# Last tiles of a dense expert mixer finished half by half, fetches paced to end earlier, nine more of them in the first pass

## Chip, core and metric

One core of one Trainium2 chip runs the whole program. The metric is the device time of one execution in microseconds, as the median of several runs. TensorE (PE) does matrix products, VectorE (DVE) and ScalarE (ACT) work on 128-partition tiles, GpSimd (POOL) issues the indirect fetches here, and SyncE (SP) issues most other DMAs.

## What is computed

A layer of token mixing is followed by an expert mixer (PEER) over 1024 latent tokens and 16384 experts with one row each in `peer_u` and `peer_v`. The changed part is the expert mixer and the final norm:

```python
def peer_ffn(h, q_w, sub_keys, u_tab, v_tab):
    ...
    top_s, pos = lax.top_k(cand_s, PEER_TOPK)
    idx = jnp.take_along_axis(cand_i, pos, axis=-1)
    gates = jax.nn.softmax(top_s, axis=-1)
    def chunk(args):
        x_c, i_c, g_c = args
        act = jax.nn.gelu(jnp.einsum('chkd,cd->chk', u_tab[i_c], x_c))
        return jnp.einsum('chk,chkd->cd', g_c * act, v_tab[i_c])
    ...
xl = xl + g2 * peer_ffn(hl2, ...)
return rmsnorm(xl, final_g)
```

Each token has 8 heads of 16 experts, so 128 of the 16384 rows count for it.

## The kernel before

The 1024 tokens are 8 tiles of 128. The experts of three of them (`GTILES` 0, 6, 7) are fetched row by row; for the five others (`DTILES` 1 to 5, 640 tokens) every expert is multiplied densely and the gates, mostly zero, select.

**Fetched tiles.** `gathered()` is a generator of 768 steps: for each tile 128 fetches from `peer_u` (`ru`, each followed by a dot product on VectorE, line 1133), then 128 from `peer_v` (`rv`, each followed by a multiply-add into `acc`, line 1144). One step is one indirect DMA on POOL (`rows()`, line 1116) of 128 rows of 1024 floats, 512 KB. Seven buffers (`UVB`) hold fetched rows. `advance(n)` brings the generator to step n, and `paced()` ties each fetch to the latest eviction of the dense work, so the fetches run in step with the products. The numbers in `PACE` set how far: 45 steps come before the first pass, `PACE["u"]` more in it.

**First pass.** For each of 128 blocks of 128 experts, `peer_ut` is loaded (`du`), split in a high part (ScalarE, `duh`) and a low part (VectorE, `dul`), multiplied with the 640 tokens on PE (`ds`, three products each, `mm3`), passed through GELU on ScalarE (`ge`), and stored to `d_ge`. In the last blocks the operands of the second pass begin to be loaded.

**Second pass.** 32 groups of 4 blocks. Per block, `operands()` (line 1218 ff.) loads `dws` from `d_ge` and `dvs` from `peer_v`, multiplies `dws` by the gates `dgs` (one load of 1.25 MB for a group), and splits both (ScalarE `dwhs`, `dvhs`; VectorE `dwls`, `dvls`). PE forms ten results of 128 x 512, two column halves of each of the five tiles, with 12 products each in a group: seven stay in PSUM banks (`stay`, shown as `dp`), and three (`dq`) share one bank, are evicted after each group and added into `dacc` by VectorE. One `advance` belongs to each of the 320 results: fetching ends `VEND` = 8 results before the end.

**The end.** In the last group the ten results are finished in the order `LAST`, and whenever both halves of a tile are there, `finish()` does its part: product with `g2b` (line 1098), addition of the residual row `x1r` (line 1099, on GpSimd for tiles in `EASED`, on VectorE for the others), square and sum on ScalarE (line 1100). The inverse roots (`rsqrt_few`, twelve small VectorE instructions, lines 148 to 154) and the final products (line 1108) come for two tiles together, and then for three (`ENDS`). The fetched tile 7 has a `finish()` of its own at the end of `gathered()`.

What each engine executes is one queue in the order that a scheduler gave it when the program was built; an instruction that waits holds everything behind it on its engine. SP's and POOL's DMA issues are such queues too.

## Time and profile before

| what | value |
| --- | --- |
| median of 3 runs | 3594.12 us (3587.15 to 3605.07) |
| the profiled execution | 3599.58 us, of which the span is 3597.6 us |
| PE busy | 3257.7 us, 91% of the span |
| VectorE busy | 2803.5 us, 78% |
| ScalarE, POOL busy | 1514.4 us (42%), 1364.3 us (38%) |
| chain that ended last | PE 36%, VectorE 5%, DMA 2%, issue 2% |
| HBM traffic | 800.64 MB read, 121.63 MB written |

The shares are means over stages: the mixing part fills the time up to about 1400 us, the first pass runs from there to about 2700 us, the second from there to 3572 us. Which engine limits a stage is read from the busy time of that stage and from what PE waits for in it. A timeline row gives start, duration, engine, line, operation, output and inputs, and, in brackets, the idle time before it and who ended it.

### The profile page before, as it was taken

The numbers are of one execution on the slowest core, as the hardware profiler recorded it, in microseconds if no ns is written. First come the engines' busy times: TensorE is split into PE (matmuls) and PEld (weight loads), VectorE is DVE, ScalarE is ACT, GpSimd is POOL, SyncE is SP. The second block draws the span as 40 slices with busy tenths as digits, with TensorE's granted clock in tenths as the row PEclk, the third lists the DMA queues.
The fourth block names the chain that finished last, engine by engine and source line by source line (L and its number), as shares of the span: only waits on it lengthen the run. The fifth ranks groups of instructions, "written<-read, shape, count | busy, mean of one in ns | idle before, by whom it ended". The sixth has DMA issues, their size and how long they took to land. (4 is left out here: it accounts for less than half of the span.)

```text
span 3597.6 us, 62347 instructions
## 1 busy us (share of the span) xinstructions
PE 3257.7 (91%) x23447; PEld 2906.9 (81%) x23447; DVE 2803.5 (78%) x6117; ACT 1514.4 (42%) x2918; POOL 1364.3 (38%) x1052
## 2 busy tenths in 40 slices
PE   6788989977788879899899999999978999999996
PEld 5566777766788668899899999999966888888885
DVE  6654554466578579798889999997769988888888
ACT  3543333232465332363436667666522333233322
POOL 3332233231111233554423335465545445444433
PEclk8899999987899889999999999999998999999998
DMA  7434435352553546999878789999999999999996
GB/s 256 139 101 141 147 105 153 93 152 78 166 157 113 181 162 230 326 321 323 298 272 279 279 285 359 359 360 352 335 350 370 372 352 350 359 344 345 356 344 235
DMA packets 404718, 926.39 MB, mean 258 GB/s; under 512 B 45504, under 2 KB 182080, under 8 KB 398784
## 3 DMA queue, kind: packets, MB, share of 16 engines
q1 hardware_dynamic: 246976, 406.71, 35.4%
q0 software_dynamic: 111920, 407.95, 31.1%
q10 hardware_dynamic: 45520, 107.76, 7.7%
q8 instruction: 184, 3.01, 0.3%
q14 instruction: 118, 0.97, 0.1%
HBM read 800.64 MB, written 121.63 MB: 256 GB/s over the span
## 5 line engine op out<-in xcount | busy, mean ns | idle before, releaser
L1116 POOL DMA_INDIRECT ru<-in_peer_u_dram,idx x384 | 519.4, 1353 | 637.2 <-ACT dqs L1350 152.9
L1116 POOL DMA_INDIRECT rv<-in_peer_v_dram,idx x384 | 502.5, 1309 | 667.2 <-ACT dqs L1350 187.3
L1144 DVE SCALAR_TENSOR_TENSOR acc<-rv,gw,acc 128x1024 f32<-128x1024 f32 x381 | 488.3, 1282 | 25.7 <-DMA rv<-in_peer_v_dram,idx 21.7
L1133 DVE CUSTOM_DVE_ANT_0 ru<-ru,h 128x1024 f32<-128x1024 f32 x384 | 461.2, 1217 | 50.5 <-DMA ru<-in_peer_u_dram,idx 50.2
L160 PE MATMUL dp<-dvls,dwhs 128*128 128x512 f32 x896 | 347.8, 391 | 0.0
L161 PE MATMUL dp<-dvhs,dwls 128*128 128x512 f32 x896 | 346.1, 390 | 0.0
L209 POOL TENSOR_TENSOR wl<-w,wh 128x1024 fp32r<-128x1024 f32 x68 | 165.7, 2439 | 385.0 <-ACT wh L207 363.8
L159 PE MATMUL dp<-dvhs,dwhs 128*128 128x512 f32 x896 | 248.7, 396 | 0.2 <-ACT dvhs L1231 0.2
L159 PE MATMUL pj<-hbh,wh 128*128 128x512 f32 (+1 forms) x544 | 216.8, 399 | 16.6 <-ACT hbh L189 14.7
L160 PE MATMUL pj<-hbl,wh 128*128 128x512 f32 (+1 forms) x544 | 212.3, 390 | 3.9 <-POOL hbl L190 3.9
L1265 ACT ACTIVATE ge<-ds 128x256 f32<-128x256 f32 (+1 forms) x256 | 110.7, 433 | 247.0 <-PE ds L161 222.6
L161 PE MATMUL pj<-hbh,wl 128*128 128x512 f32 (+1 forms) x544 | 211.1, 388 | 2.3 <-POOL wl L209 2.3
L159 PEld LDWEIGHTS dp<-dvhs,dwhs 128*128 128x128 f32 x896 | 171.5, 192 | 36.2 <-ACT dvhs L1231 0.6
L160 PEld LDWEIGHTS dp<-dvls,dwhs 128*128 128x128 f32 x896 | 169.3, 189 | 35.4
L161 PEld LDWEIGHTS dp<-dvhs,dwls 128*128 128x128 f32 x896 | 169.2, 189 | 35.3
L1235 ACT CAST dwhs<-dws 128x640 fp32r<-128x640 f32 x128 | 91.9, 730 | 233.5 <-DVE dws L1234 205.0
L159 PE MATMUL dq<-dvhs,dwhs 128*128 128x512 f32 x384 | 152.1, 396 | 32.6 <-ACT dvhs L1231 26.0
L727 POOL TENSOR_TENSOR kl<-kd,kh 128x768 fp32r<-128x768 f32 (+1 forms) x24 | 55.0, 2290 | 319.2 <-ACT kh L725 293.0
L1231 ACT CAST dvhs<-dvs 128x1024 fp32r<-128x1024 f32 x128 | 134.0, 1051 | 91.6 <-DMA dvs<-in_peer_v_dram 91.5
L207 ACT CAST wh<-w 128x1024 fp32r<-128x1024 f32 x68 | 71.0, 1046 | 234.6 <-PE pj L160 169.8
L1350 ACT COPY dqs<-dq 128x512 f32<-128x512 f32 x90 | 52.8, 587 | 276.9 <-PE dq L161 276.9
L1048 PE MATMUL gm<-oa,ob 128*128 128x128 f32 x1280 | 159.1, 277 | 3.6 <-DVE oa L1035 3.0
(1980 smaller groups left out, 10123.5 us busy)
## 6 DMA issues: line engine op xcount, KB each, us to landing
du<-in_peer_ut_dram SPq DMA_DIRECT2D x128, 512.0 KB, 6.4
dvs<-in_peer_v_dram SPq DMA_DIRECT2D x128, 512.0 KB, 7.0
d_ge<-ge ACTq DMA_DIRECT2D x128, 320.0 KB, 5.4
d_g<-gt ACTq DMA_DIRECT2D x40, 1024.0 KB, 10.5
dgs<-d_g SPq DMA_DIRECT2D x32, 1280.0 KB, 9.4
dws<-d_ge SPq DMA_DIRECT2D x128, 320.0 KB, 8.2
w<-in_w_in_dram SPq DMA_DIRECT2D x68, 512.0 KB, 3.6
wq<-in_q_w_dram SPq DMA_DIRECT2D x48, 512.0 KB, 4.0
```

What stands on the lines that cost most here:

```text
L159: nc.tensor.matmul(ps, lh_, rh_, start=start, stop=False)
L160: nc.tensor.matmul(ps, lh_, rl_, start=False, stop=False)
L161: nc.tensor.matmul(ps, ll_, rh_, start=False, stop=stop)
L207: nc.scalar.copy(wh, w)
L209: WE[0].tensor_tensor(wl, w, wh.bitcast(F32), op=OP.subtract)
L1048: nc.tensor.matmul(ps[:, t * P:(t + 1) * P], ob[:, q + t], oa[:, q + t], start=True, stop=True)
L1116: paced(nc.gpsimd.indirect_dma_start(out=r, out_offset=None, in_=A[tab], in_offset=bass.IndirectOffsetOnAxis(ap=idx[:, tt, s:s + 1], axis=0)))
L1133: yield from rows("peer_u", tt, lambda s, u: nc.vector.tensor_tensor_reduce(u, u, h2, 1.0, 0.0, OP.mult, OP.add, act[:, s:s + 1]))
L1144: nc.vector.scalar_tensor_tensor(acc, v, w[:, s:s + 1], acc, op0=OP.mult, op1=OP.add)
L1231: nc.scalar.copy(vh, v)
L1235: nc.scalar.copy(wh, wt)
L1265: ev = nc.scalar.activation(ge[:, t0:t0 + n], ps, AF.Gelu_apprx_tanh)
```

## The change

Three numbers change and the end is rewritten.

- `PACE["u"]` goes from 450 to 459: nine more fetch steps in the first pass, nine fewer in the second.
- `VEND` goes from 8 to 17: fetching ends nine results sooner. In the second pass 288 steps (with the 15 of `LAG`) over 312 results become 279 over 303.
- In the last group each half of a dense tile is finished as soon as its products are done (`half_done`): product with `g2b`, addition of `x1r` (on VectorE always), square and sum of 512 columns on ScalarE. The second half of a tile adds the two sums, takes one inverse root for that tile, and does the final product and the store to HBM in two halves. GpSimd adds nothing any more, and `ENDS` and `EASED` are gone.

```diff
--- before.py
+++ after.py
@@ -38,15 +38,13 @@
 GROUPS = ((0, 256), (256, 512), (768, 256))
 DBLK = ((0, 256), (256, 384))
 EB, VB = 4, 7
-PACE = dict(g0=5, g1=(40,), u=450)
+PACE = dict(g0=5, g1=(40,), u=459)
 REST = (16, 2)
 HTOK, TOKS, IBLK = 32, 8, 64
 GSTEPS = TD // TOKS
-VEND = 8
+VEND = 17
 SEAM = 6
-ENDS = ((0, 4), (1, 2, 3))
 LAG = 15
-EASED = (1, 5, 7)
 LAST = (7, 0, 8, 1, 9, 2, 3, 4, 5, 6)
 HP = (600, 500)
 BESIDE = 1.2
@@ -1086,8 +1084,6 @@
         sm, accs = pl.tile([P, 2 * n], F32, tag=f"sm{n}", name=f"sm{tts[0]}", bufs=2), []
 
         def wide(nm, tt):
-            if late and nm == "fin" and tt in DTILES:
-                return late[2][DTILES.index(tt)]
             return ex.tile([P, D], F32, tag="uv", name=f"{nm}{tt}", bufs=UVB)
 
         for i, tt in enumerate(tts):
@@ -1096,7 +1092,7 @@
             for q, part in enumerate(parts[i]()):
                 d_ = slice(q * 512, (q + 1) * 512)
                 nc.vector.tensor_mul(acc[:, d_], part, g2b[:, d_])
-            (nc.gpsimd if late and tt in EASED else nc.vector).tensor_add(acc, acc, x1r)
+            nc.vector.tensor_add(acc, acc, x1r)
             nc.scalar.activation(x1r, acc, AF.Square, accum_out=sm[:, i:i + 1])
             accs.append(acc)
             yield
@@ -1300,6 +1296,27 @@
 
     old = dgs[NGRP % 2].rearrange("p c i t -> p (c i t)")
     late.append([old[:, :D], old[:, D:2 * D], dqs.rearrange("p a b -> p (a b)")] + fins_)
+
+    def half_done(got, i):
+
+        (t, q), part = divmod(i, 2), stay[i] if i < len(stay) else dacc[:, i - len(stay)]
+        tt, d_ = DTILES[t], slice(q * 512, (q + 1) * 512)
+        both = t in got
+        if not both:
+            x1r = ex.tile([P, D], F32, tag="uv", name=f"x1r{tt}", bufs=UVB)
+            nc.sync.dma_start(x1r, d_x1[tt * P:(tt + 1) * P, :])
+            got[t] = (x1r, late[2][t], dn.tile([P, 4], F32, tag="smd", name=f"smd{tt}", bufs=TD // P))
+        x1r, acc, sm = got[t]
+        nc.vector.tensor_mul(acc[:, d_], part, g2b[:, d_])
+        nc.vector.tensor_add(acc[:, d_], acc[:, d_], x1r[:, d_])
+        nc.scalar.activation(x1r[:, d_], acc[:, d_], AF.Square, accum_out=sm[:, q:q + 1])
+        if both:
+            nc.vector.tensor_add(sm[:, 2:3], sm[:, 0:1], sm[:, 1:2])
+            rsqrt_few(dn, sm[:, 3:4], sm[:, 2:3], 1, 1e-6, 1.0 / D, "fn1")
+            for d_ in (slice(0, 512), slice(512, D)):
+                nc.vector.scalar_tensor_tensor(acc[:, d_], acc[:, d_], sm[:, 3:4], late[0][:, d_], op0=OP.mult, op1=OP.mult)
+                nc.sync.dma_start(out[tt * P:(tt + 1) * P, d_], acc[:, d_])
+
     for g in range(NGRP):
         if g:
             ws.clear()
@@ -1322,7 +1339,7 @@
         left_ = GT * 2 * P - n1
         steps = NGRP * NT2 - VEND
         if g == NGRP - 1:
-            fins, fgen, ends = (), None, list(ENDS)
+            got = {}
             for x, i in enumerate(LAST):
                 if i < len(stay):
                     acc_of(i, stay[i], False, True)
@@ -1331,15 +1348,7 @@
                     acc_of(i, ps, True, True)
                     nc.vector.tensor_add(dacc[:, i - len(stay)], ps, dacc[:, i - len(stay)])
                 advance(n1 - LAG + (g * NT2 + x + 1) * (left_ + LAG) // steps)
-                if (i ^ 1) in LAST[:x]:
-                    if not fins:
-                        fins = ends.pop(0)
-                        fgen = finish([DTILES[t] for t in fins], [lambda t=t: [stay[j] if j < len(stay) else dacc[:, j - len(stay)] for j in (2 * t, 2 * t + 1)] for t in fins])
-                    assert fins[0] == i // 2
-                    next(fgen)
-                    fins = fins[1:]
-                    if not fins:
-                        drain(fgen)
+                half_done(got, i)
             break
         for r in range(nr):
             ps = bank(f"dq{g}{r}", "ch")
```

What the scheduler makes of it shows in three places. In the rows, the number behind an underscore is a buffer's serial number.

The first is VectorE at the end. Before, the last three fetched rows (`rv7_125` to `rv7_127`) stand between the finishing steps of the dense tiles and ahead of the addition of the ninth result (`dq318`):

```order
L1098 TENSOR_TENSOR dgs0_27653<-dp3_28065,g2b_9644 128x512
L1144 SCALAR_TENSOR_TENSOR acc7_31320<-rv7_125_33797,gw7_31317,acc7_31320 128x1024
L1098 TENSOR_TENSOR dqs_28082<-dp4_28066,g2b_9644 128x512
L1144 SCALAR_TENSOR_TENSOR acc7_31320<-rv7_126_33843,gw7_31317,acc7_31320 128x1024
L1144 SCALAR_TENSOR_TENSOR acc7_31320<-rv7_127_33858,gw7_31317,acc7_31320 128x1024
L1332 TENSOR_TENSOR dacc_28069<-dq318_33861,dacc_28069 128x512
L1098 TENSOR_TENSOR fin7_33893<-acc7_31320,g2b_9644 128x512 x2
L1098 TENSOR_TENSOR dqs_28082<-dp5_28067,g2b_9644 128x512
L1098 TENSOR_TENSOR fin1_28084<-dacc_28069,g2b_9644 128x512
L1098 TENSOR_TENSOR fin0_28083<-dp6_28068,g2b_9644 128x512
L1332 TENSOR_TENSOR dacc_28069<-dq319_33923,dacc_28069 128x512
```

Now the last fetched rows stand ahead of the last group's operands (`dvls0`, `dvls1`), and tile 7 is finished (`fin7`) before the last group's products:

```order
L1140 SCALAR_TENSOR_TENSOR acc7_31162<-rv7_125_33707,gw7_31159,acc7_31162 128x1024
L1360 TENSOR_TENSOR dacc_28096<-dqs_28109,dacc_28096 128x512
L1140 SCALAR_TENSOR_TENSOR acc7_31162<-rv7_126_33710,gw7_31159,acc7_31162 128x1024
L1140 SCALAR_TENSOR_TENSOR acc7_31162<-rv7_127_33713,gw7_31159,acc7_31162 128x1024
L1094 TENSOR_TENSOR fin7_33761<-acc7_31162,g2b_9644 128x512 x2
L1228 TENSOR_TENSOR dvls0_27687<-dvs0_27683,dvhs0_27686 128x1024
L1095 TENSOR_TENSOR fin7_33761<-fin7_33761,x1r7_33760 128x1024
L1232 TENSOR_TENSOR dwls1_27689<-dws1_27682,dwhs1_27688 128x640
L1228 TENSOR_TENSOR dvls1_27691<-dvs1_28114,dvhs1_27690 128x1024
```

Fetched rows have left the stretch in which the dense tiles are finished.

Behind the last result (`dq319`, the tenth) VectorE has now the following; the roots of two tiles (`smd5` and `smd2`) then alternate instruction by instruction:

```order
L1349 TENSOR_TENSOR dacc_28096<-dq319_33957,dacc_28096 128x512
L152 SCALAR_TENSOR_TENSOR smd1_33898<-fn1t_33940,fn1y_33939 128x1
L1314 TENSOR_TENSOR smd3_34061<-smd3_34061 128x1
L1314 TENSOR_TENSOR smd4_33880<-smd4_33880 128x1
L1310 TENSOR_TENSOR fin1_28111<-dacc_28096,g2b_9644 128x512
L1317 SCALAR_TENSOR_TENSOR dgs0_27680<-dgs0_27680,smd1_33898,fgs_28088 128x512 x2
L1311 TENSOR_TENSOR fin1_28111<-fin1_28111,x1r5_33916 128x512
L1314 TENSOR_TENSOR smd5_33918<-smd5_33918 128x1
L146 TENSOR_SCALAR fn1a_33975<-smd5_33918 128x1
L146 TENSOR_SCALAR fn1a_34028<-smd2_34008 128x1
```

The five dense tiles' final products (`L1108` before, 1024 columns each) have become halves that stand behind the root of their own tile.

The second place is SP's queue between the passes. Before, after the last `dvs` loads of group 0, the gates of group 1 (`dgs1`) come first and the load of its first block (`dws1`) behind them:

```order
L1218 DMA dvs0_27656<-in_peer_v_dram 128x1024 x2
L1218 DMA dgs1_28085<-d_g_79 128x20x128
L1218 DMA dws1_27655<-d_ge_78 128x640
L1218 DMA dvs0_27656<-in_peer_v_dram 128x1024
L1218 DMA dws2_28086<-d_ge_78 128x640
L1218 DMA dvs1_28087<-in_peer_v_dram 128x1024
```

Now three loads of group 1 stand ahead of its gates:

```order
L1214 DMA dvs0_27683<-in_peer_v_dram 128x1024 x2
L1214 DMA dws1_27682<-d_ge_78 128x640
L1214 DMA dvs0_27683<-in_peer_v_dram 128x1024
L1214 DMA dws0_27681<-d_ge_78 128x640
L1214 DMA dgs1_28112<-d_g_79 128x20x128
L1214 DMA dws2_28113<-d_ge_78 128x640
```

The gates of group 1 have moved back behind `dws1`, `dvs0` and `dws0`.

The third is ScalarE at the end of the first pass. Before, the high part of block 124 is cast behind the second GELU of block 123:

```order
L1265 ACTIVATE ge122_27594<-ds122_256_27621 128x384
L1267 DMA d_ge_78<-ge122_27594 128x640
L1059 CAST du123h_27692<-du123_27690 128x1024
L1265 ACTIVATE ge123_27696<-ds123_0_27697 128x256
L1265 ACTIVATE ge123_27696<-ds123_256_27723 128x384
L1267 DMA d_ge_78<-ge123_27696 128x640
L1059 CAST du124h_27771<-du124_27769 128x1024
```

Now it is cast together with that of block 123:

```order
L1261 ACTIVATE ge122_27621<-ds122_256_27648 128x384
L1263 DMA d_ge_78<-ge122_27621 128x640
L1057 CAST du123h_27719<-du123_27717 128x1024
L1057 CAST du124h_27798<-du124_27796 128x1024
L1261 ACTIVATE ge123_27723<-ds123_0_27724 128x256
L1261 ACTIVATE ge123_27723<-ds123_256_27750 128x384
```

The cast `du124h` has moved ahead of both evictions of block 123.

The nine added fetches of the first pass show on VectorE by how far the rows of tile 6 have come when a block is split. Before, at the last block (`du127l`):

```order
L1144 SCALAR_TENSOR_TENSOR acc6_25016<-rv6_60_26725,gw6_25013,acc6_25016 128x1024
L1236 TENSOR_TENSOR dwls3_27670<-dws1_27655,dwhs3_27669 128x640
L1144 SCALAR_TENSOR_TENSOR acc6_25016<-rv6_61_26818,gw6_25013,acc6_25016 128x1024
L1061 TENSOR_TENSOR du127l_28000<-du127_27996,du127h_27998 128x1024
L1144 SCALAR_TENSOR_TENSOR acc6_25016<-rv6_62_26821,gw6_25013,acc6_25016 128x1024
```

Now:

```order
L1140 SCALAR_TENSOR_TENSOR acc6_24812<-rv6_67_26746,gw6_24809,acc6_24812 128x1024
L1140 SCALAR_TENSOR_TENSOR acc6_24812<-rv6_68_26749,gw6_24809,acc6_24812 128x1024
L1140 SCALAR_TENSOR_TENSOR acc6_24812<-rv6_69_26842,gw6_24809,acc6_24812 128x1024
L1059 TENSOR_TENSOR du127l_28027<-du127_28023,du127h_28025 128x1024
L1140 SCALAR_TENSOR_TENSOR acc6_24812<-rv6_70_26845,gw6_24809,acc6_24812 128x1024
```

VectorE is eight fetched rows further there (`rv6_69` against `rv6_61`). Counted in the same way, blocks 0 to 33 have no lead, blocks 34 to 104 one of two to six rows, and from block 105 on it swings between two to four and five to eight.

## Rows read from the trace of the kernel before

**Rows 1.** busy us per engine in long stretches, granted clock, DMA share, GB/s
```profile
core 0: us, PE busy (x) PEld busy (x) DVE busy (x) ACT busy (x) POOL busy (x), PEclk, DMA share, GB/s
1950.00:2425.00 475.00, 474.95 (x3458) 474.44 (x3458) 464.30 (x999) 324.99 (x764) 215.21 (x152) 1.00 0.89 326
2600.00:2830.00 230.00, 195.85 (x916) 164.53 (x916) 184.33 (x181) 59.18 (x81) 108.29 (x85) 0.93 1.02 362
2830.00:3560.00 730.00, 726.62 (x3200) 600.43 (x3200) 627.52 (x781) 224.56 (x292) 331.92 (x250) 1.00 0.98 346
```

**Rows 2.** two tens of the tail, columns as in Rows 1
```profile
3570.00:3580.00 10.00, 2.44 (x11) 1.69 (x9) 10.00 (x12) 4.53 (x8) 7.53 (x3) 0.80 0.20 66
3580.00:3590.00 10.00, 0.00 (x0) 0.00 (x0) 9.65 (x38) 2.23 (x4) 0.87 (x1) 0.50 0.26 107
```

**Rows 3.** PE timeline, last products: start, us, what, [idle before <-releaser]
```profile
3569.43 0.50 PE L159 MATMUL dq<-dvhs,dwhs 128*128 128x512 f32 x1 [1.69 <-DVE dacc L1332]
...
3572.05 0.39 PE L161 MATMUL dq<-dvhs,dwls 128*128 128x512 f32 x1
```

**Rows 4.** VectorE timeline of the tail, columns as in Rows 3
```profile
3559.59 1.28 DVE L1144 SCALAR_TENSOR_TENSOR acc<-rv,gw,acc 128x1024 f32<-128x1024 f32 x1 [2.10 <-DMA rv<-in_peer_v_dram,idx]
...
3561.39 1.88 DVE L1098 TENSOR_TENSOR dgs<-dp,g2b 128x512 f32<-128x512 f32 x3
...
3577.46 1.21 DVE L1099 TENSOR_TENSOR dqs<-dqs,x1r 128x1024 f32<-128x1024 f32 x1
...
3578.65 3.30 DVE L1099 TENSOR_TENSOR fin<-fin,x1r 128x1024 f32<-128x1024 f32 x1
...
3584.90 0.15 DVE L153 SCALAR_TENSOR_TENSOR fn2t<-fn2t,fn2a 128x2 f32<-128x2 f32 x1
...
3586.36 0.16 DVE L153 SCALAR_TENSOR_TENSOR fn3t<-fn3t,fn3a 128x3 f32<-128x3 f32 x1
...
3590.91 1.28 DVE L1108 SCALAR_TENSOR_TENSOR dqs<-dqs,sm,fgs 128x1024 f32<-128x1024 f32 x1
3592.11 1.28 DVE L1108 SCALAR_TENSOR_TENSOR fin<-fin,sm,fgs 128x1024 f32<-128x1024 f32 x1
```

**Rows 5.** GpSimd timeline of the tail: its last addition
```profile
3577.60 3.27 POOL L1099 TENSOR_TENSOR fin<-fin,x1r 128x1024 f32<-128x1024 f32 x1 [1.82 <-issue]
```

**Rows 6.** ScalarE timeline of the tail: a square and its sum
```profile
3581.99 1.06 ACT L1100 ACTIVATE x1r<-fin 128x1024 f32<-128x1024 f32 x1
3582.95 0.19 ACT L1100 ACTIVATION_READ_ACCUMULATOR x1r<-fin 128x1 f32 x1
```

**Rows 7.** VectorE timeline, first pass, blocks 36 and 37
```profile
1767.25 1.23 DVE L1061 TENSOR_TENSOR du36l<-du,du36h 128x1024 fp32r<-128x1024 f32 x1 [1.53 <-ACT du36h L1059]
...
1771.10 1.22 DVE L1061 TENSOR_TENSOR du37l<-du,du37h 128x1024 fp32r<-128x1024 f32 x1 [2.22 <-ACT du37h L1059]
1772.24 2.60 DVE L1144 SCALAR_TENSOR_TENSOR acc<-rv,gw,acc 128x1024 f32<-128x1024 f32 x2
```

**Rows 8.** PE's waits, 2600 to 2830 us: total, times, longest
```profile
PE dq L159 <- ACT dvhs L1231: 26.0, 5, 13.3
PE ds L159 <- ACT du124h L1059: 2.1, 1, 2.1
```

**Rows 9.** SP's DMA queue between the passes: start, us, DMAs issued
```profile
2678.70 0.38 SPq L1218 DMA_DIRECT2D dgs<-d_g  x1
2679.13 10.62 SPq L1218 DMA_DIRECT2D dws<-d_ge  x1
```

**Rows 10.** VectorE timeline between the passes
```profile
2700.50 0.83 DVE L1234 TENSOR_TENSOR dws<-dws,dgs 128x640 f32<-128x640 f32 x1 [12.71 <-DMA dws<-d_ge]
```

**Rows 11.** POOL timeline between the passes: fetches
```profile
2669.84 1.86 POOL L1116 DMA_INDIRECT rv<-in_peer_v_dram,idx  x1 [3.50 <-DVE acc L1144]
...
2688.90 0.93 POOL L1116 DMA_INDIRECT rv<-in_peer_v_dram,idx  x1 [0.30 <-issue]
2708.15 1.28 POOL L1116 DMA_INDIRECT rv<-in_peer_v_dram,idx  x1 [18.31 <-DVE acc L1144]
```

## The prediction

> **What bounds the kernel now.** I read the busy time of each engine in long stretches first, then two tens of us at the end, then the timelines of PE and VectorE there, and last PE's waits between the two passes. [...] Between the passes PE loses 230 - 195.85 = 34.2 us [rows 1]; 26.0 of them are five waits for a cast operand of the second pass, the longest 13.3 us [rows 8]. At the end PE stops and VectorE is the bound: it is busy for 10.00 and 9.65 us of two tens while PE falls to 2.44 and 0 [rows 2]. PE's last product ends at 3572.05 + 0.39 = 3572.44 us [rows 3], VectorE's last instruction at 3592.11 + 1.28 = 3593.39 [rows 4], the span at 3597.6. So 25.2 us lie behind the last product, 21.0 of them VectorE's and 4.2 the last stores and the close.
>
> The change can therefore gain in three places only: in those 25.2 us, in what VectorE makes PE wait for just before them, and between the passes. Taking nine fetches out of the second pass as such gains nothing, since PE is full there.
>
> **The tail, term by term.** First PE. The tenth result waited 1.69 us for VectorE's addition of the ninth [rows 3], because multiply-adds of fetched rows stood ahead of it, and these in turn waited for their DMAs (2.10 us before one of them, [rows 4]). In the new order all fetched rows stand ahead of the last group's operands, and a fetch schedule that ends nine results earlier (12 products each, one every 2.62/11 = 0.24 us [rows 3], so some 25 us) leaves them time to land. Between the first and the tenth result of the last group VectorE now has 20 instructions of 512 columns and 13 small ones, 20 x 0.60 + 13 x 0.10 = 13.3 us by the spacings below, while PE has 64 products, 15.2 us. VectorE is not late at the last product, by a reserve of 1.9 us. That takes 1.7 us off PE's end (a wait of 0.2 us for the ninth result goes too, which I leave out).
>
> Then VectorE behind the last product. A 1024-column instruction starts 3592.11 - 3590.91 = 1.20 us after the one before it [rows 4], and three of 512 columns take 1.88 us together, which is 3 x 0.60 + 0.08. Small instructions of two alternating roots start every (3586.36 - 3584.90)/15 = 0.097 us [rows 4]. By the new order there are behind the last result: one addition, one product with `g2b`, one addition of `x1r` and ten half products, 13 x 0.60 = 7.8 us; 52 small ones, 52 x 0.097 = 5.0; and one stop, while ScalarE squares the last half. A square of 1024 columns takes 1.06 us and the read of its sum 0.19 [rows 6]; I take 0.6 + 0.2 = 0.8 for the half, an estimate from these. Sum 13.7 with the last instruction's 0.08. With the same 4.2 us for stores and close, 17.9 us instead of 25.2: a gain of 7.3. Together with PE's 1.7 the tail gives **-9.0 us**.
>
> What has left the stretch: the last fetched rows, tile 7's finish, and GpSimd's additions. A GpSimd addition of 1024 columns took 3.27 us [rows 5], and the VectorE addition that ran beside it 3.30 instead of 1.21 [rows 4]; now every addition costs VectorE 2 x 0.60. What has come: ten more squares and sums in halves on ScalarE, which was idle there, and ten stores instead of five.
>
> Bounds: if the roots do not alternate and each small instruction takes its own 0.16 us [rows 4], 52 of them cost 3.3 us more, and half products at half of 1.28 us cost 0.5 more, and VectorE's reserve of 1.9 may be missing. That leaves 9.0 - 5.7 = 3.3 us. On the other side the last store is half as large; if the 4.2 us shrank by half the gain would be 11.1.
>
> [...] In the rows, halves queued behind each other cost no more than a whole, 2 x 0.60 against 1.20 [rows 4]. [...]
>
> **The nine fetches in the first pass.** Each brings one multiply-add of 1.30 us on VectorE (two took 2.60, [rows 7]) and a transfer of 512 KB. By the order they enter at two places: three around blocks 34 to 37, the others in the last blocks. At the first place VectorE stood idle for 1.53 and 2.22 us, waiting for ScalarE's casts [rows 7]; 3 x 1.30 = 3.9 fit into these 3.75 but for 0.15. At the second VectorE has 184.33 of 230 us [rows 1]. In the full stretch between, the lead stays as it is, so nothing is added there. I take 0. Without this cover it is 9 x 1.30 = 11.7 us; a gain is excluded in the body, since PE has no idle time to give back there.
>
> **Between the passes.** Two moves in the queues. ScalarE now casts `du124h` with `du123h`, ahead of two evictions of block 123, so PE's wait for it, 2.1 us [rows 8], goes: **-2.1** (0 if the load is late).
> Against it, SP now issues `dvs0` (512 KB) and `dws0` (320 KB) ahead of group 1's gates (1280 KB), where `dws1` only changes sides. This is the place of PE's longest wait: gates and `dws1` were issued at 2678.70 and 2679.13 [rows 9], VectorE stood 12.71 us for them until 2700.50 [rows 10], ScalarE's casts stood behind VectorE, and PE behind those. 1600 KB took 21.8 us there, 73 KB per us, because POOL issued 14 fetches of 512 KB from 2669.84 to 2688.90 [rows 11]. The 832 KB more cost 832/73 = 11.3 us at that rate, or 832/362 = 2.3 at the rate of the whole stretch, 362 GB/s [rows 1]. What is behind VectorE here: all multiply-adds of fetched rows, and with their buffers full POOL stops (18.31 us, [rows 11]). I take **+3**, near the lower end, because POOL's fetches stop at 2688.90 and whatever is still due comes at the full rate.
>
> **Sum:** -9.0 + 0 - 2.1 + 3 = -8.1 us. Against the profiled execution 3599.6 - 8.1 = 3591.5; this lay 5.5 us above the median, so for the median 3594.1 - 8.1 = **3586**. With the bounds of all terms the forecast's own case reaches from 3594.1 - 11.1 - 2.1 + 2.3 = 3583 to about 3592.
>
> **Rivals.**
> *Group 1's gates come at the low rate.* The move costs 11.3 instead of 3: 3594, no change. For it: the fetch stream is eight rows further on VectorE but as dense; the DMA share is 1.02 there. Against: the stop of the fetches.
> *VectorE pays for the fetches in the first pass* and ends on the other side. Its queue is 98% full from 1950 to 2425 us; if the lead is made up there in time, not in order, every added multiply-add pushes a `dul` back and PE waits: +11.7, 3594.1 - 8.1 + 11.7 = 3598. It is slower than before from seven unhidden rows on (8.1/1.30 = 6.2). Against it: PE waited for nearly nothing there, so its operands have some lead.
> *The waits between the passes rearrange in our favour.* Three loads of group 1 come earlier, so the wait of 13.3 us may shrink and the later ones go. If 13 of the 26.0 us vanish and the 3 are not paid, 3586 - 16 = 3570.
> *The tail does not shorten as counted*, because VectorE is late at the last product or the roots do not alternate: a gain of 3.3, 3592.
>
> **How the numbers follow.** Forecast 0.55, short tail gain 0.10, gates late 0.14, first pass 0.11, rearranged 0.10. Half a per cent, about what a measurement of this kernel can tell from no change, is 18 us: below 3576 or above 3612. Only the rearranged case reaches below, 0.10, and a little of the forecast by the spread of runs (18 us between the fastest and the slowest of before), 0.02. Above 3612 both costly cases have to come together, 0.06. So faster 0.12, same 0.82, slower 0.06. The range for 8 in 10 goes from 3574, which takes in part of the rearranged case, to 3601, which takes in both single costly cases with the spread.
>
> **What would show it.** Right: PE's end to the end of the span is 17 to 20 us; no wait of PE for `dacc` in the last ten products; no GpSimd addition; VectorE's small instructions in pairs 0.1 us apart; no wait for `du124h`; one wait of 13 to 18 us before group 1. Wrong: a tail of 22 us or more, with gaps on VectorE between the halves; PE below 470 of 475 us in the body of the first pass with waits for `dul`; or a sum of PE's waits between the passes that differs from 34 us by more than 8, which would decide the time in place of the tail.

## The result and the profile after

The changed kernel takes **3615.11 us** in the median (8 runs) where the kernel before takes 3596.36 (8 runs): a ratio of **1.0054, interval 1.0039 to 1.0069**. It is slower by half a per cent, 19 us; the forecast was 3586 in a range of 3574 to 3601. The profiled execution took 3616.15 us, its span is 3614.4 us.

The end came out as counted. First PE's last product, then VectorE behind it (timeline, columns as in [rows 3] and [rows 4]):

```profile
3595.47 0.39 PE L159 MATMUL dq<-dvhs,dwls 128*128 128x512 f32 x1
```

```profile
3596.64 0.68 DVE L1349 TENSOR_TENSOR dacc<-dq,dacc 128x512 f32<-128x512 f32 x1
...
3597.74 0.68 DVE L1310 TENSOR_TENSOR fin<-dacc,g2b 128x512 f32<-128x512 f32 x1
3598.34 1.41 DVE L1317 SCALAR_TENSOR_TENSOR dgs<-dgs,smd,fgs 128x512 f32<-128x512 f32 x2
3599.66 0.68 DVE L1311 TENSOR_TENSOR fin<-fin,x1r 128x512 f32<-128x512 f32 x1
3601.14 0.16 DVE L1314 TENSOR_TENSOR smd<-smd 128x1 f32<-128x1 f32 x1 [0.79 <-ACT x1r L1312]
3601.33 0.21 DVE L146 TENSOR_SCALAR fn1a<-smd 128x1 f32<-128x1 f32 x2
...
3609.80 1.41 DVE L1317 SCALAR_TENSOR_TENSOR fin<-fin,smd,fgs 128x512 f32<-128x512 f32 x2
```

PE's last product ends at 3595.47 + 0.39 = 3595.86, VectorE at 3609.80 + 1.41 = 3611.21, the span at 3614.4: 18.5 us behind the last product instead of 25.2. PE has no wait for `dacc` in the last group (1.69 us in [rows 3]), the small instructions stand in pairs, and VectorE's stop for ScalarE is 0.79 us. But PE's last product ends **23.4 us later** than before (3572.44, [rows 3]). The long stretches, as in [rows 1]:

```profile
1950.00:2425.00 475.00, 471.68 (x3433) 471.09 (x3432) 463.15 (x999) 324.79 (x763) 207.70 (x151) 1.00 0.89 324
2600.00:2830.00 230.00, 198.06 (x947) 169.38 (x946) 184.87 (x195) 58.42 (x81) 114.68 (x85) 0.93 1.01 363
2830.00:3560.00 730.00, 718.13 (x3112) 584.95 (x3110) 614.36 (x755) 221.50 (x287) 319.48 (x241) 1.00 0.96 341
```

From 2830 to 3560 us PE is busy for 718.13 us and not 726.62, with 3112 products and not 3200, while the DMA share is lower (0.96, before 0.98). The second pass, whose length the prediction took as unchanged, is where the time went. PE's waits between 2830 and 3130 us (who waited for whom, us in total, times, longest):

```profile
PE dq L157 <- ACT dvhs L1227: 3.9, 2, 3.3
PE dq L157 <- ACT dqs L1359: 2.8, 3, 1.4
PE dq L158 <- DVE dvls L1228: 2.3, 3, 1.8
PE dp L157 <- ACT dvhs L1227: 0.9, 1, 0.9
```

Before there were 1.4 us there. The longest dvhs wait, on the queues of SP, POOL, ScalarE, VectorE and PE (timeline):

```profile
3002.99 0.37 SPq L1214 DMA_DIRECT2D dgs<-d_g  x1
3006.04 6.05 SPq L1214 DMA_DIRECT2D dvs<-in_peer_v_dram  x2
3012.18 3.39 SPq L1214 DMA_DIRECT2D dws<-d_ge  x3
3027.01 1.61 SPq L1214 DMA_DIRECT2D dvs<-in_peer_v_dram  x2
...
3014.46 1.58 POOL L1112 DMA_INDIRECT ru<-in_peer_u_dram,idx  x1 [0.30 <-issue]
3035.22 1.27 POOL L1112 DMA_INDIRECT ru<-in_peer_u_dram,idx  x1 [19.19 <-ACT dqs L1359]
...
3024.68 1.04 ACT L1227 CAST dvhs<-dvs 128x1024 fp32r<-128x1024 f32 x1 [11.27 <-DMA dvs<-in_peer_v_dram]
...
3025.76 2.51 DVE L1228 TENSOR_TENSOR dvls<-dvs,dvhs 128x1024 fp32r<-128x1024 f32 x2 [7.30 <-ACT dvhs L1227]
...
3025.78 0.50 PE L157 MATMUL dq<-dvhs,dwhs 128*128 128x512 f32 x1 [3.30 <-ACT dvhs L1227]
```

And three stretches around it, the third inside the second (busy times as in [rows 1], then granted clock, DMA share, GB/s):

```profile
3000.00:3020.00 20.00, 20.00 (x89) 16.36 (x88) 17.25 (x26) 5.89 (x8) 8.51 (x7) 1.00 1.03 372
3020.00:3040.00 20.00, 16.70 (x66) 13.26 (x66) 13.52 (x18) 5.30 (x6) 3.99 (x3) 0.91 0.55 189
3026.00:3029.00 3.00, 3.00 (x9) 2.32 (x9) 2.94 (x3) 1.01 (x1) 0.00 (x0) 0.58 0.27 89
```

Two loads of `peer_v` are issued from 3006.04, right behind 1.25 MB of gates. ScalarE stands 11.27 us for them, VectorE 7.30, PE 3.30. SP can issue no further `dvs` until VectorE has freed one of the two buffers (3027.01), POOL no fetch until PE's next eviction (19.19 us). So the DMA engines, at a share of 1.03 in the 20 us ahead, stand at 0.55 in the next: nobody may issue. PE's own wait is 3.30 us, but it does 66 products there instead of 89: the granted clock was 0.91 in these 20 us and 0.58 from 3026 to 3029 us, behind the wait, where it does 9 products in 3 us. The chain that ended last goes through that load and others (start, length, what):

```profile
2855.24 11.98 DMA dws<-d_ge
...
2924.18 9.09 DMA dws<-d_ge
...
2964.61 11.70 DMA dvs<-in_peer_v_dram
...
3006.04 18.62 DMA dvs<-in_peer_v_dram
```

In the chain of before no load of an operand stands behind 2830 us.

### The profile page after: what moved, and what is told of

The parts are those of the page before. It is cut to its first block, busy times and chain, and to the rows that moved or that the text cites. A ratio compares the mean times of both kernels' runs of the same rounds, so it can differ in the third digit from the quotient of the medians.

```text
span 3614.4 us, 62423 instructions
## 1 busy us (share of the span) xinstructions
PE 3281.5 (91%) x23447; PEld 2920.3 (81%) x23447; DVE 2807.3 (78%) x6171; ACT 1515.8 (42%) x2928; POOL 1350.6 (37%) x1049
## 5 line engine op out<-in xcount | busy, mean ns | idle before, releaser
L1112 POOL DMA_INDIRECT ru<-in_peer_u_dram,idx x384 | 510.1, 1328 | 653.5 <-ACT dqs L1359 163.7
L157 PE MATMUL dp<-dvhs,dwhs 128*128 128x512 f32 x896 | 263.8, 395 | 0.9 <-ACT dvhs L1227 0.9
L157 PE MATMUL pj<-hbh,wh 128*128 128x512 f32 (+1 forms) x544 | 218.2, 401 | 16.7 <-ACT hbh L187 14.7
L157 PE MATMUL dq<-dvhs,dwhs 128*128 128x512 f32 x384 | 152.2, 396 | 27.1 <-ACT dwhs L1231 11.2
L1228 DVE TENSOR_TENSOR dvls<-dvs,dvhs 128x1024 fp32r<-128x1024 f32 x128 | 155.6, 1219 | 21.0 <-ACT dvhs L1227 20.8
## 6 DMA issues: line engine op xcount, KB each, us to landing
d_g<-gt ACTq DMA_DIRECT2D x40, 1024.0 KB, 11.7
```

The source lines that it names most:

```text
L157: nc.tensor.matmul(ps, lh_, rh_, start=start, stop=False)
L1112: paced(nc.gpsimd.indirect_dma_start(out=r, out_offset=None, in_=A[tab], in_offset=bass.IndirectOffsetOnAxis(ap=idx[:, tt, s:s + 1], axis=0)))
L1228: sv = nc.vector.tensor_tensor(vl, v, vh.bitcast(F32), op=OP.subtract)
```

## Experiments

Eighteen kernels were run. In the table: the ratio to the kernel before; from the profiled execution the length of the first pass (from `du0l`, the first split on VectorE, to group 0), the first eviction of the second pass (group 0, `dacc<-dq` on ScalarE), from there to the end of PE's last product, the part of that between the first evictions of groups 2 and 12 (`dqs<-dq`), the issue of the last fetch on POOL, and what lies behind PE's last product.

| kernel | ratio (interval) | first pass | group 0 at | to PE's end | groups 2 to 12 | last fetch at | behind PE |
| --- | --- | --- | --- | --- | --- | --- | --- |
| before | 1 | 1290.6 | 2680.3 | 892.2 | 275.1 | 3557.3 | 25.2 |
| after | 1.0054 (1.0039 to 1.0069) | 1295.1 | 2684.7 | 911.2 | 298.3 | 3563.2 | 18.5 |
| e1_half_alone | 1.0032 (1.0019 to 1.0046) | 1291.3 | 2684.5 | 906.0 | 282.9 | 3572.3 | 24.0 |
| e2_half_v17 | 1.0032 (1.0016 to 1.0048) | 1285.6 | 2682.3 | 913.1 | 290.3 | 3562.1 | 16.8 |
| e3_u459_only | 1.0020 (1.0007 to 1.0033) | 1299.5 | 2694.6 | 890.1 | 283.3 | 3570.1 | 26.9 |
| e4_after_u458 | 1.0058 (1.0036 to 1.0080) | 1298.2 | 2698.9 | 915.1 | 293.0 | 3580.3 | 16.7 |
| e5_half_pad | 0.9997 (0.9982 to 1.0013) | 1288.6 | 2680.5 | 895.9 | 279.4 | 3560.6 | 25.5 |
| e6_before_shift | 1.0015 (1.0002 to 1.0027) | 1279.8 | 2663.5 | 900.9 | 280.4 | 3547.8 | 25.1 |
| e7_after_pad | 1.0045 (1.0029 to 1.0060) | 1299.0 | 2687.9 | 910.3 | 295.7 | 3566.1 | 19.0 |
| e8_half_v17_pad | 1.0030 (1.0017 to 1.0043) | 1282.3 | 2673.3 | 910.7 | 292.2 | 3551.3 | 16.7 |
| e9_before_light | 0.9987 (0.9974 to 1.0000) | 1284.9 | 2683.6 | 896.2 | 266.5 | 3557.4 | 19.2 |
| e10_after_light | 0.9956 (0.9939 to 0.9973) | 1295.5 | 2688.1 | 883.8 | 263.1 | 3526.6 | 13.5 |
| e11_half_g49 | 1.0004 (0.9987 to 1.0021) | 1299.7 | 2700.5 | 893.8 | 282.5 | 3562.3 | 19.1 |
| e12_half_g58 | 1.0035 (1.0019 to 1.0051) | 1324.3 | 2709.9 | 878.7 | 272.0 | 3554.3 | 17.1 |
| e13_after_d3 | 1.0026 (1.0011 to 1.0041) | 1295.1 | 2686.6 | 900.9 | 279.6 | 3553.7 | 17.7 |
| e14_v17_d3 | 0.9969 (0.9950 to 0.9987) | 1285.3 | 2678.5 | 888.7 | 280.5 | 3534.0 | 18.2 |
| e15_half_d3 | 0.9983 (0.9967 to 0.9998) | 1286.0 | 2672.4 | 884.8 | 276.1 | 3544.0 | 26.3 |
| e16_before_d3 | 0.9985 (0.9966 to 1.0003) | 1293.2 | 2687.7 | 881.1 | 276.2 | 3556.7 | 28.0 |
| e17_v17_d3w4 | 0.9999 (0.9988 to 1.0009) | 1284.4 | 2677.5 | 875.3 | 269.8 | 3560.3 | 43.6 |
| e18_after_d3w4 | 0.9986 (0.9976 to 0.9996) | 1302.1 | 2695.0 | 873.2 | 270.6 | 3555.6 | 29.3 |

One profile says little about the time up to group 0: before, e1_half_alone, e5_half_pad and e6_before_shift have the same queues up to the last 40 products, and reach it between 2663.5 and 2684.5. The stretch behind it repeats better.

**The parts one by one.** The first question was which of the changed numbers or the new end moves PE's end. There are two such numbers, `PACE["u"]` and `VEND`, not three.

The first two are edits of the changed kernel, the third of the kernel before, the fourth of the changed one:

```diff
-PACE = dict(g0=5, g1=(40,), u=459)
+PACE = dict(g0=5, g1=(40,), u=450)
-VEND = 17
+VEND = 8
```

```diff
-PACE = dict(g0=5, g1=(40,), u=459)
+PACE = dict(g0=5, g1=(40,), u=450)
```

```diff
-PACE = dict(g0=5, g1=(40,), u=450)
+PACE = dict(g0=5, g1=(40,), u=459)
```

```diff
-PACE = dict(g0=5, g1=(40,), u=459)
+PACE = dict(g0=5, g1=(40,), u=458)
```

> The new end alone: dense tiles finished by halves, but 450 fetch steps in the first pass and fetching ending 8 results before the end, as before. Theory A (the nine fetches in the first pass re-sort the queues between the passes and cost PE's 23 us): PE ends where it did before, 3572 us give or take 4, about 19 to 22 us lie behind its last product, and the time is 3 to 7 us under the kernel before. Theory B (the earlier end of fetching costs it): the same here. Theory C (the new end itself re-sorts the second pass): PE ends 15 to 25 us later than before, and the time is 8 to 18 us over the kernel before.

> The new end and the earlier end of fetching (17 results before the end), with 450 fetch steps in the first pass as before: 303 steps over 303 results in the second pass, 1.00 a result instead of 0.97. Theory A (the nine fetches in the first pass cost it): PE ends within 4 us of before, 18 to 19 us lie behind it, the time is 6 to 10 us under the kernel before. Theory B (the earlier end or the denser second pass costs it): PE ends 15 us or more after before, and the time is 8 us or more over the kernel before.

> Only the nine more fetch steps in the first pass (459); fetching ends 8 results before the end, and the old end stands. In the second pass 294 steps over 312 results, 0.94 a result. Theory A: PE ends 15 to 25 us later than before, with waits of 9 us and more in sum between 2760 and 3050 us; with the old end of 25 us the time is 15 to 25 us over the kernel before. Theories B and C: PE ends within 4 us of before and so does the time.

> The changed kernel with one fetch step less in the first pass (458). If the nine fetches cost by their load (VectorE's multiply-adds, transfers), this kernel is within 3 us of the changed one, 3612 us, or 0.5% over the kernel before. If they cost because every other number sorts the queues between the passes anew, it can come out 10 us or more away from the changed kernel, on either side, with other waits of PE between 2600 and 3050 us; the end still takes 18 to 19 us behind PE's last product.

No theory came out whole. The new end alone was slower by 0.32%, which theories A and B excluded and C asked for; 459 alone by 0.20%, half of what A asked, with PE's end 12 us later where C allowed 4. One step less (458) made no difference to the time of the changed kernel. That is one neighbour only, and the queues between the passes did change with it (49.4 us from group 0 to group 1 instead of 41.4), so it doesn't exclude that each number deals the queues anew. The expectations count the 15 steps of `LAG` twice in their fetches per result: by the kernel these are 0.92 in before and in the changed kernel, 0.95 in e2 and 0.89 in e3. The surprise is e1: its order of instructions on every engine is that of before up to the last 40 products, and yet its second pass is 14 us longer.

**The place of the buffers.** The new end needs fewer small tiles. The pool that holds operand slots 4 to 6, `dacc`, `dqs`, `dgs1`, `dws2` and `dvs1` is 352 bytes smaller and stacked from above, so all of these begin at a multiple of 64 bytes, where before they began 32 over one. Padding restores or moves that: 88 columns in e5, e7 and e8, which are e1, the changed kernel and e2 with it, and 8 columns in e6, which is the kernel before.

```diff
     dvs[1] = dn.tile([P, D], F32, name="dvs1")
+    dn.tile([P, 88], F32, name="pad")
```

> The new end alone, as in e1_half_alone, whose queues are in the order of before up to the last 40 products, with 352 unused bytes added to the pool that holds the buffers of the second pass, so that operand slots 4 to 6, dqs, dacc, dgs1, dws2 and dvs1 lie at the addresses of before again. Theory P (place: the smaller pool moved these buffers by 352 bytes, from 32 over a multiple of 64 bytes to a multiple of 64, and products and transfers became slower by it): the spacing of the products between 3150 and 3310 us returns from 0.2285 to 0.227 us, PE ends 12 to 17 us sooner than in e1_half_alone, and the time is 3590 to 3596 us, 3 to 8 us under the kernel before. Rival Q (the 17 us of e1_half_alone are another effect of the new end, or chance): like e1_half_alone, 10 to 14 us over the kernel before.

> The kernel before with 32 unused bytes in the same pool, nothing else: the buffers of the second pass move from 32 over a multiple of 64 bytes to a multiple of 64. Theory P: spacing of the products of 0.228 to 0.230 us in the steady part of the second pass, PE's end 10 to 17 us later, the time 0.3 to 0.5% over the kernel before. Rival Q: no change, within 4 us.

> The changed kernel with 352 unused bytes in the same pool, so that the buffers of the second pass lie where they did before. Theory P: 10 to 17 us of the changed kernel's 17 to 19 go, 3597 to 3606 us, and what is left to the kernel before with its end 7 us shorter, some 5 to 12 us, is the price of the nine fetches by the new order of the queues between the passes. Rival Q: unchanged, 0.4 to 0.6% over the kernel before.

> The new end and the earlier end of fetching (17 results before the end) with 450 steps in the first pass, as e2_half_v17, with 352 unused bytes so that the buffers of the second pass lie where they did before. Theory P: 10 to 17 us under e2_half_v17, 3590 to 3602 us; if fetching at 1.00 a result instead of 0.97 costs nothing, 6 to 10 us under the kernel before, with 18 us behind PE's last product. Rival Q: as e2_half_v17, 0.3% over the kernel before.

The steady part shows it best. ScalarE's first eviction in groups 12 and 28, for before, e5_half_pad, e1_half_alone and e6_before_shift:

```profile
3040.73 0.59 ACT L1350 COPY dqs<-dq 128x512 f32<-128x512 f32 x1 [4.28 <-PE dq L161]
...
3479.82 0.59 ACT L1350 COPY dqs<-dq 128x512 f32<-128x512 f32 x1 [6.39 <-PE dq L161]
```

```profile
3044.26 0.59 ACT L1360 COPY dqs<-dq 128x512 f32<-128x512 f32 x1 [4.27 <-PE dq L159]
...
3483.36 0.59 ACT L1360 COPY dqs<-dq 128x512 f32<-128x512 f32 x1 [6.38 <-PE dq L159]
```

```profile
3052.24 0.59 ACT L1359 COPY dqs<-dq 128x512 f32<-128x512 f32 x1 [4.53 <-PE dq L159]
...
3494.78 0.59 ACT L1359 COPY dqs<-dq 128x512 f32<-128x512 f32 x1 [6.45 <-PE dq L159]
```

```profile
3028.63 0.59 ACT L1351 COPY dqs<-dq 128x512 f32<-128x512 f32 x1 [4.50 <-PE dq L161]
...
3470.63 0.59 ACT L1351 COPY dqs<-dq 128x512 f32<-128x512 f32 x1 [6.46 <-PE dq L161]
```

Sixteen groups take 439.09 and 439.10 us with the buffers 32 over a multiple of 64, and 442.54 and 442.00 on one: 0.2 us a group, 6 us in 31 groups. Between 3040 and 3480 us PE is equally busy in all four and waits equally (2.7 us, for `dqs`), and does fewer products in e1 and e6; before, e5, e1 and e6:

```profile
3040.00:3480.00 440.00, 437.30 (x1925) 361.02 (x1924) 378.31 (x442) 136.39 (x178) 193.63 (x148) 1.00 1.00 349
```

```profile
3040.00:3480.00 440.00, 437.30 (x1926) 360.92 (x1925) 378.15 (x444) 136.59 (x177) 193.66 (x148) 1.00 0.99 349
```

```profile
3040.00:3480.00 440.00, 437.30 (x1910) 357.84 (x1909) 374.95 (x445) 136.69 (x177) 190.46 (x147) 1.00 0.98 347
```

```profile
3040.00:3480.00 440.00, 437.30 (x1914) 358.47 (x1913) 376.73 (x438) 135.91 (x176) 189.85 (x147) 1.00 0.99 349
```

By the times, e6 is 0.15% over before (5 us) and e1 0.35% over e5 (13 us, with intervals wide enough for 6). Theory P holds for the steady part of these pairs, and not for the 10 to 17 us that it asked; a third pair agrees there (e2 446.24 us, e8 442.98). For the changed kernel it doesn't show: e7 takes back 0.09% only, and its sixteen groups take 447.17 us against 444.07, with 5.9 us of PE's waits instead of 1.4. By the time, e8 takes back nothing that can be told. Most of the loss is something else.

**Are the transfers behind it?** The DMA share from 3040 to 3480 us is 1.00 in the kernel before, as shown above (0.98 in [rows 1] with the last groups in it). Two kernels move less: e9 is the kernel before and e10 is e7, both with the gates of groups 0 and 1 used to the end. They leave out 30 loads, so they don't compute the layer; only their time is of use.

```diff
-            vload(g, dgs[g % 2], d_g[...])
+            if g < 2:
+                vload(g, dgs[g % 2], d_g[...])
```

> The kernel before, but the gates dgs of groups 2 to 31 are not loaded: the second pass uses those of groups 0 and 1 again, which leaves out 30 x 1.25 of some 9.5 MB that a group moves, 13%. Theory D (the transfers bound the second pass as much as PE does; a fetch moved forward pushes PE back): the DMA share between 3150 and 3500 us falls from 1.00 to 0.85 to 0.90, PE's period stays 27.2 us a group, the waits in groups 2 to 12 shrink, and the time is 5 to 20 us under the kernel before. Rival O (the waits come from the order of the queues): the time and the waits in groups 2 to 12 stay, within 4 us.

> The changed kernel with its buffers at the old addresses, as e7_after_pad, and the gates of groups 2 to 31 not loaded, as in e9_before_light. Theory D: with the transfers relieved, the earlier end of fetching costs PE nothing, so that this kernel is no longer 16 us over its counterpart but within 8 us of e9_before_light on either side (the end 6 to 7 us shorter, the nine fetches of the first pass up to 12 us dearer), and PE's last product comes 24 us or less behind the last fetch's issue only because it is paced so. Rival O: still 14 us or more over e9_before_light, with waits of 15 us and more in groups 2 to 12.

The share falls to 0.85 and 0.86 as expected, but the relief gives the kernel before only 0.13%, 5 us at the edge of theory D: its second pass is not shorter (896.2 us), since new waits come behind 3150 us (PE busy 342.58 of the 350 us to 3500, before 347.98). Relieved in the same way, the changed kernel wins: 0.9956 against 0.9987, 11 us under its counterpart, where with all gates it is 16 us over; theory D asked for 8 us on either side, rival O for 14 over. The stretch from 2830 to 3130 us of e7_after_pad and of e10_after_light (busy times of PE, weight load, VectorE, ScalarE, POOL, then clock, DMA share, GB/s):

```profile
2830.00:3130.00 300.00, 289.26 (x1254) 236.84 (x1254) 243.45 (x355) 89.02 (x116) 132.07 (x99) 0.99 0.94 335
```

```profile
2830.00:3130.00 300.00, 300.00 (x1326) 248.39 (x1325) 271.97 (x402) 96.90 (x128) 150.50 (x110) 1.00 0.90 324
```

Not a wait of PE is left there. One caution: leaving loads out also changes the order of the queues, so this pair does not part load from order.

**Fetches still earlier.** If the second pass is full, nine fetches might go in front of the first one (e8 with 49 steps there, and with 58).

```diff
-PACE = dict(g0=5, g1=(40,), u=450)
+PACE = dict(g0=5, g1=(49,), u=450)
```

> The new end, the earlier end of fetching (17) and the old addresses, but the nine fetch steps that leave the second pass go in front of the first one (49 instead of 40 beside the last mixing products, 450 in the first pass as before), where the DMA share is 0.77 to 0.93 and VectorE 88% busy. Theory D, with the nine fetches free at that place: the second pass has 0.97 fetches a result, PE ends 0 to 6 us later than before, the end is 17 to 19 us, the time 2 to 8 us under the kernel before. If the nine cost there too (VectorE), or if fetches at 0.97 a result with the earlier end still push PE back by the 16 to 20 us of e7_after_pad and e8_half_v17_pad: 5 to 15 us over the kernel before.

> As e11_half_g49 with 18 more fetch steps in front of the first pass instead of nine: 0.94 fetches a result in the second pass, as many as in e3_u459_only, which gained 0.2 us a group on the kernel before there. Theory D: the last fetch is issued some 10 us sooner than in e11_half_g49, PE's end follows it, and the time is 3 to 10 us under e11_half_g49. Otherwise (VectorE pays 1.3 us for each of the 18 in the mixing part): 10 us over e11_half_g49.

Both shorten the second pass against e8 (910.7 to 893.8 and 878.7 us) and reach it later, at 2700.5 and 2709.9: what is taken from the one is paid ahead of it, in the first pass (1299.7 and 1324.3 us, 1282.3 in e8). In the kernel before, the 90 us ahead of the first pass (1300 to 1390 us) have VectorE busy for 83.19 us and a DMA share of 0.60, where the expectation of e11 has 88% and 0.77 to 0.93. No gain over the kernel before: 1.0004 lies between the two ranges expected of e11, and 18 steps are dearer than nine, where theory D had them cheaper. But e11 shows something else. It has as many fetches in the second pass as e7, the same end of fetching and two buffers for `dvs`, and from 2830 to 3130 us PE has no wait at all (300.00 us busy, 289.26 in e7).

**The loop of two loads.** In e7 the DMA share from 2830 to 3130 us is lower than before (0.94, before 1.01) while PE waits for transfers, as in the 20 us shown above. So a third buffer for `dvs` (one of the tiles kept for the end) in four kernels:

```diff
-        v = dvs[e % 2 if g else 0]
+        v = dvs[e % 3 if g else 0]
...
+    dvs.extend(fins_[:1])
```

> The changed kernel with its buffers at the old addresses (e7_after_pad), and a third buffer for the loads of peer_v in the second pass (the first of the two tiles kept for the end, fin0, serves until then). Theory L (a loop of two loads in flight: SP waits for VectorE's dvls to free a buffer, the load lands late, ScalarE and VectorE and PE wait): the waits of PE between 2830 and 3130 us (10.7 us in e7_after_pad) fall under 3, the DMA share there rises from 0.94 to 0.99 or more, PE ends 10 us or more sooner, and the time is 8 to 18 us under e7_after_pad, near the kernel before or under it. Rival D (the DMA engines are full, so an operand is late whatever the number of buffers): the waits and the time as in e7_after_pad, 0.3 to 0.5% over the kernel before.

> The same third buffer in e8_half_v17_pad (new end, fetching ends 17 results before the end, 450 steps in the first pass). Theory L: the waits of 10.5 us between 2830 and 3130 us go, PE's end comes 10 us sooner, and with the end of 17 us the time is 0 to 8 us under the kernel before. Rival D: 0.2 to 0.4% over it, as e8_half_v17_pad, with a drift of 0.2 to 0.3 us a group from 1.00 fetches a result.

> The same third buffer in e5_half_pad (the new end alone, old addresses), which has hardly a wait between 2830 and 3130 us (1.4 us), but 29 us of waits for dvhs and dvls between 2600 and 2830. Theory L: these shrink by 5 us or more, and the time is 3 to 10 us under the kernel before. Rival D: no change, within 4 us of it.

> The same third buffer in the kernel before, with nothing else changed. Theory L: 3 to 10 us under the kernel before, by the waits for dvhs between 2600 and 2830 us (26.0 us). Rival D: no change, within 4 us. It is also the counterpart that tells what of e13_after_d3, e14_v17_d3 and e15_half_d3 belongs to the buffer alone.

All four are faster than the same kernel with two: by 0.19, 0.61, 0.14 and 0.15%, of which 0.61 is beyond the intervals and the others agree in sign. ScalarE's wait for these loads between 2830 and 3130 us, in before, after, e8_half_v17_pad, e13_after_d3 and e14_v17_d3:

```profile
ACT dvhs L1231 <- DMA dvs<-in_peer_v_dram: 22.8, 10, 4.4
```

```profile
ACT dvhs L1227 <- DMA dvs<-in_peer_v_dram: 60.8, 25, 11.3
```

```profile
ACT dvhs L1227 <- DMA dvs<-in_peer_v_dram: 39.9, 11, 10.2
```

```profile
ACT dvhs L1227 <- DMA dvs<-in_peer_v_dram: 2.6, 2, 1.7
```

```profile
ACT dvhs L1227 <- DMA dvs<-in_peer_v_dram: 4.9, 3, 2.7
```

The wait that the changed kernel had nearly trebled is gone, as theory L says. In e13 the share rises to 0.99 as expected, but PE still waits 10.6 us between 2830 and 3130 us, now for `dwhs`, and the gain is 7 us and not 8 to 18. **e14_v17_d3 beats both kernels**: 3587.10 us in the median, 0.31% under before and 0.85% under the changed one. With the wider loop the new end and the earlier end of fetching are no longer a loss: 0.9969 against 0.9985 in e16, which has neither, though these intervals overlap. The nine fetches in the first pass are a loss still: e13, which is e14 with 459 steps, is 0.57% over it.

The waits for `dwhs` hang on three buffers of loads from `d_ge`; the last two kernels have four.

```diff
-        wt = dws[e % (3 if g else 2)]
+        wt = dws[e % (4 if g else 2)]
...
+    dws.append(fins_[1][:, :TD])
```

> e14_v17_d3 (new end, fetching ends 17 results before the end, 450 steps in the first pass, old addresses, three dvs buffers) with a fourth buffer for the loads from d_ge (the second of the tiles kept for the end, fin1, serves until then). Theory L at both loads: PE's waits for dwhs and dqs between 2830 and 3500 us (8.7 us) go, and the time is 3 to 8 us under e14_v17_d3, 0.4 to 0.5% under the kernel before. Rival D (with three dvs buffers the transfers are the bound, share 1.00): as e14_v17_d3, 0.2 to 0.4% under the kernel before.

> e13_after_d3 (the changed kernel with 459 steps, old addresses, three dvs buffers) with the same fourth dws buffer. Theory L at both loads: PE's waits for dwhs between 2830 and 3500 us (22.0 us in e13_after_d3) fall under 8, and the time is 10 to 20 us under e13_after_d3, at or under the kernel before. Rival F (the 459 steps cost by themselves: VectorE's nine multiply-adds of 1.30 us in the full first pass, or the order): the waits go or move but the time stays over e17_v17_d3w4 by 10 us or more.

PE has no wait over 0.9 us from 2830 to 3500 us in either, and its second pass is the shortest of all: 875.3 and 873.2 us. With 459 steps that gives 0.40% against e13. By its sign rival F fails, since e18 is not over e17; but that doesn't clear the 459 steps, whose first pass takes 1302.1 us in e18 and 1284.4 in e17. With 450 it costs 0.30% against e14. Why, the end of e17 shows, PE, POOL and VectorE:

```profile
3552.39 0.39 PE L159 MATMUL dq<-dvhs,dwls 128*128 128x512 f32 x1
```

```profile
3560.25 1.02 POOL L1112 DMA_INDIRECT rv<-in_peer_v_dram,idx  x1 [0.30 <-issue]
```

```profile
3555.22 10.53 DVE L1140 SCALAR_TENSOR_TENSOR acc<-rv,gw,acc 128x1024 f32<-128x1024 f32 x8
...
3569.69 1.29 DVE L1094 TENSOR_TENSOR fin<-acc,g2b 128x512 f32<-128x512 f32 x2
```

PE is done 20 us sooner than before, and the last fetch is issued 7 us behind it. VectorE adds fetched rows until 3569.69 and finishes all but the first steps of the tiles behind that. The fetches became the end; that the operands' loads took their turn ahead of them is inferred, not shown.

## Why the prediction was wrong

**The tail: right in size, half right in cause.** 18.5 us against 17.9 counted, and no wait of the tenth result: -6.6 of the forecast -7.3, and the -1.7. Two sizes were off and nearly cancel. VectorE needs 15.4 us behind PE's end instead of 13.7, the stores and the close 3.2 instead of 4.2. The reserve of 1.9 us was missing: tile 7's root and final product kept VectorE until 3583.21, 2.1 us after the first result of the last group was ready (3580.72 + 0.39), and it came to the tenth 0.8 us behind PE's end. And two of the final half products take 1.32 us (3598.34 to 3599.66), not 1.20.

e5_half_pad, with the new end and fetching up to 8 results before the end, has 25.5 us behind PE and its time is that of before. In its rows multiply-adds of fetched rows stand among the halves until 3575 us, and tile 7 is finished behind them. So halves and single roots gained nothing there. The gain comes with the earlier end of the fetches: 25.5 to 16.7 from e5 to e8, where `VEND` alone changes. From e3 to e7 (26.9 to 19.0) the new end changes too. The earlier end with the old finish was not run, so what the halves add to it is open; e9, with the old finish and fewer bytes to move, has 19.2.

**Halves against their spacing in the rows.** In the row at 3597.74 a half product lasts 0.68 us and the next instruction starts 0.60 behind it, as the rows of before let expect; the final products above stand 0.66 apart. The 0.68 us, here and for the addition at 3599.66, is the duration of one instruction, 0.60 the distance of two in a full queue.

**Nine fetches in the first pass: the step "I take 0" failed.** The first pass takes 1295.1 to 1302.1 us in the six kernels with 459 steps (after, e3, e7, e10, e13, e18) and 1279.8 to 1293.2 in the eleven with 450 and none added ahead of it (before, e1, e2, e5, e6, e8, e9, e14 to e17). On average that is 11 us, close to the 9 x 1.30 = 11.7 of the rival in which VectorE pays, and the pass begins at the same time in both (1391.8 and 1392.0 us on average). Before and after, VectorE and ScalarE:

```profile
1389.72 1.22 DVE L1061 TENSOR_TENSOR du0l<-du,du0h 128x1024 fp32r<-128x1024 f32 x1
...
2680.28 0.59 ACT L1348 COPY dacc<-dq 128x512 f32<-128x512 f32 x1 [6.13 <-PE dq L161]
```

```profile
1389.56 1.21 DVE L1059 TENSOR_TENSOR du0l<-du,du0h 128x1024 fp32r<-128x1024 f32 x1
...
2684.70 0.59 ACT L1357 COPY dacc<-dq 128x512 f32<-128x512 f32 x1 [8.49 <-PE dq L159]
```

The rival had the place wrong, though. From `du36l` to `du104l`, the full stretch of VectorE, the two sets differ by under 1 us on average, as the prediction said. The loss is 3 us between `du30l` and `du36l` and 10 us between `du104l` and `du127l`, of which 3 come back by group 0: the two places where it saw room, 3.75 us of stops and 184.33 of 230 us. Five pairs differ in the 459 alone. It costs 0.20% from before to e3, 0.22 from e2 to after, 0.15 from e8 to e7 and 0.57 from e14 to e13; from e17 to e18, where fetches are the end, it gains 0.13.

**Between the passes: +1 was counted, -9 came.** From group 0 to group 1 before takes 50.8 us, after 41.4, e3 41.3, e7 41.1. The wait for `du124h` is gone, as forecast; the other loads of group 1 that now stand ahead of its gates helped instead of hurting: the longest wait fell from 13.3 us [rows 8] to 11.2. So the prices of two rivals came true at once, and they nearly cancel (+11 on average and -9). That left the sum as it was, and was luck.

**The body of the second pass: the step that decided.** The prediction said that taking fetches out of it gains nothing, "since PE is full there", and counted the earlier end of fetching only where it helps the tail. It asked nothing more of the body, and none of its signs of being wrong looked there; none of them came (a tail of 18.5 us, 471.68 us in the first pass, 31.9 us without PE between the passes). [rows 1] had the answer beside it: DMA share 0.98 with PE at 726.62 of 730. Two resources were full, and the operands reach PE over a loop with two loads in flight.

In the two profiles the spans differ by 16.8 us: 4.4 up to group 0, -9.4 from there to group 1, **28.4 from group 1 to PE's last product** (841.3 and 869.7 us), and -6.6 behind it. Of the 28.4, 23.2 come between groups 2 and 12 (275.1 and 298.3 us) and 5.0 between groups 12 and 28. The latter in the changed kernel, 444.07 us against the 439.09 above:

```profile
3059.80 0.58 ACT L1359 COPY dqs<-dq 128x512 f32<-128x512 f32 x1
...
3503.87 0.59 ACT L1359 COPY dqs<-dq 128x512 f32<-128x512 f32 x1 [3.82 <-PE dq L159]
```

Between groups 2 and 12 lie the late `dvs` loads and the low clock behind the waits (0.58 in the 3 us from 3026 above). Some 5 us of the 23 belong to this one profile of before, which is that much shorter there than e1, e5 and e6 with the same queues up to the last 40 products.

Which edit brings it? With two `dvs` buffers, 45 steps ahead of the first pass and all loads, the five kernels that end fetching 17 results before the end (after, e2, e4, e7, e8) take 290 to 298 us there, and the five that end it 8 before (before, e1, e3, e5, e6) 275 to 283. From e5 to e8 `VEND` alone changes, and it costs 0.33%, 12 us; in the profiles the way to PE's end grows by 14.8 us and the tail shrinks by 8.8. From e15 to e14, with three buffers, the same edit costs nothing (0.9983 and 0.9969). So with two buffers, at this pacing, the earlier end of fetching costs the second pass more than the tail gains. Along one path of single edits the ratios give the whole: the new end at the old addresses -0.03% (e5), the earlier end 0.33 (e8), nine fetches 0.15 (e7), the addresses 0.09 (after). Each of these is known to some 0.2% only, and another path shares them out otherwise, as e1 shows (new end and addresses together, 0.32).

How much the transfers can move at most is not shown: the traces have 349 GB/s at a DMA share of 1.00 from 3040 to 3480 us before, and 372 at 1.03 in the 20 us from 3000 after.

**Still open.** Third and fourth buffers and fewer bytes each take the waits for `dvs` away, and each changes the order of the queues as well. And e11, with two buffers and the earlier end, has none of them and takes 282.5 us for groups 2 to 12, so these two alone don't bring the waits: where in the queues the fetches stand decides too. The cause is thus shown as far as the earlier end and the loop, not to the single row of the queue. Why buffers at a multiple of 64 bytes cost PE 0.2 us a group is not shown either.
